# Chunked first stage, last gate on VectorE, and the order of work in the attention's tail and the second norm of a two-layer diffusion transformer

## The chip, the core and the metric

The kernel runs on one core of a Trainium2 chip. The engines are named as the profile names them: PE (TensorE, matrix products; PEld is its weight load), DVE (VectorE), ACT (ScalarE), POOL (GpSimd) and SP (SyncE, which here only issues transfers). The metric is the device time of one execution in microseconds.

## The reference

Two layers over 256 latent and 256 context tokens of 1024 columns. Each layer has a mixer (layer 0: retention with 4 heads; layer 1: neighbourhood attention with 32 heads) and an MLP of 4096 hidden columns. Six vectors per layer, shift, scale and gate for mixer and MLP, come from the condition `c` by a product with `ada_w` (adaLN).

```python
for i in range(DEPTH):
    mod = (silu_c @ ada_w[i] + ada_b[i])[:, None, :]
    mod_c = silu_cc @ ada_w[i] + ada_b[i]
    sh1, sc1, g1, sh2, sc2, g2 = jnp.split(mod, 6, axis=-1)
    ...
    h = x * (1.0 + sc1) + sh1
    hc = ctx * (1.0 + sc1c) + sh1c
    ...                                   # y, yc: retention (i = 0) or neighbourhood attention (i = 1)
    x = layer_norm(DN_ALPHA * x + g1 * y, ln_g[i, 0], ln_b[i, 0])
    h = x * (1.0 + sc2) + sh2
    x = layer_norm(DN_ALPHA * x + g2 * sq_relu_mlp(h, mlp_w1[i], mlp_w2[i]), ln_g[i, 1], ln_b[i, 1])
    if not last:
        ...                               # the same for ctx
```

Everything is float32.

## The kernel before

**Products.** A float32 operand is held as two parts that PE takes in its faster float32r form: a high part (`hi`, `hTh`: an ACT cast) and a low part (`lo`, `hTl`: DVE takes the high part from the raw value). A product is three matmuls, high x high, low x high, high x low (`mm3`). Weights are streamed by SP's queue in units of 512 KB. `fetch` loads a unit into one of four buffers (`raw`; the background's adaLN weights `rawa` use the same four) and casts it (`hi`, five buffers), `lows` makes the low parts that are still outstanding (`lo`, five buffers), `take` gives the next unit to its user. PSUM has eight banks (`bank`).

**Order.** Engines are called through wrappers (`pe`, `act`, `dve`, `pool`, `sp`). Where a wrapper's `on` is true, its instructions stay in the order in which they are written; elsewhere a scheduler orders them. Nearly every instruction is recorded at the wrapper's line, 84 before and 89 in the changed kernel, so rows are told apart by tile names.

**First stage** (to about 66 us). The shift and scale of layer 0 are made by quarters of 256 columns: `quarter_loads` brings the `ada_w` columns (`rawq`, 1-KB pieces) and the same columns of `x` and `ctx` (`R`), `quarter_rows` sums them over the 1024 rows of `ada_w` on PE (`pada`, with `cT` as the condition) and adds the biases on DVE (`row`, `brows`), `ada_columns` turns the row into columns by a small matmul with a constant (`mod`). A chunk is 128 columns: `chunk` transposes it (`pt`), `modulate_chunk` scales and shifts it, half on DVE and half on ACT, into `aff`, and `split` makes `hTh` and `hTl`. `quarter_q` and `quarter_v` accumulate the chunk's products into q (`pq`, two banks) and v (`pv`, four banks) of the first retention head. `crow` holds the rows of `c`, `c_ctx`, `ln_g` and `ln_b`, and one transpose turns them all (`pc`). `make_strip` builds the decay masks of the heads on ACT and DVE.

**Background adaLN.** The other shifts, scales and gates are made beside the main work by a generator that `bg(n)` advances by n steps. In a step DVE adds a 128x1024 slab of weights, times a column of the condition, to `acc` (`acc<-rawa,scol`), and after eight slabs PE folds the partitions (`pada<-acc,onecol`). For the two parts named in `on_pe` PE sums the slabs directly instead (`pada<-rawa,cT`); the last one, the gate of layer 1's MLP, is taken in steps 5 to 8 of the attention (`ADA`). `bg_max` limits how far the generator goes: to 79 steps in the first layer's MLP.

**Attention of layer 1** (810 to 1010 us). `STEPS` lists what goes with each step of heads: scores (`pqk`), `soften` (softmax, `s`), `flip` and `invert` (transposes `ppt`, `pt`; reciprocals of the sums, `rr`), `attend` (`pav`), `turned` (ACT's copy `rt<-pav` of the reciprocals, and what follows from it), and the output projection `wo` (`pnw`) where its heads are ready. The last two steps and the start of the projection are written out singly.

**Second norm of layer 1** (1010 to 1043 us). The two 128-token tiles are normalised one after the other. `direct` modulates the transposed tile straight from PSUM (`hTh`, and again as `aff` for `hTl`), `tok_part` makes the first MLP products of a tile by operand part (`p00`, `p01` for tile 0), `tok_block` all three parts of a block in turn (`p10`, `p11` for tile 1), `activate` squares the positive part and `turn_block` transposes it.

Of the kernel before, what the change touches and what calls it, by code (L numbers as in the profile page):

```python
# [39 lines left out]
def make_consts():  # L40
# [14 lines left out]
    add("sel", sel)  # L55
    inv = f(1.0) / (f(10000.0) ** (np.arange(0, 128, 2, dtype=f) / f(128.0)))
# [8 lines left out]
    add("pad", np.zeros((P, -sum(q.shape[1] for q in parts) % LINE)))  # L65
# [39 lines left out]
def kernel(  # L105
# [83 lines left out]
    for i in range(4):  # L189
        w_rows(WI, 256 * i, 256, 0, 256)  # L190
        w_rows(WI, 256 * i, 256, 2 * D, 512)
# [103 lines left out]
    cst = cpool.tile([P, CONSTS.shape[1]], F32, tag="cst", name="cst")  # L295
    crow = scr("crow")[:, :P]
    sp.dma_start(out=crow[0:8, :], in_=c.rearrange("a (k p) -> (a k) p", p=P))
    act.dma_start(out=crow[8:16, :], in_=c_ctx.rearrange("(k p) -> k p", p=P))
    sp.dma_start(out=cst[:], in_=consts)
    act.dma_start(out=crow[16:48, :], in_=ln_g.rearrange("l i (k p) -> (l i k) p", p=P))  # L300
    act.dma_start(out=crow[48:80, :], in_=ln_b.rearrange("l i (k p) -> (l i k) p", p=P))

    def cv(name, p0=0, p1=P):
        o, w = CONST_COLS[name]
        return cst[p0:p1, o : o + w]
# [6 lines left out]
    pc = bank("pc")  # L312
    pe.transpose(pc[:, 0:80], crow[0:80, :], ident[0:80, 0:80])
    act.activation(out=scol[:].rearrange("p a k -> p (a k)"), in_=pc[:, 0:16], func=AF.Silu)
    for t in range(2):
        dve.tensor_copy(
            out=cT[:, :, :, t], in_=scol[:, t, :].unsqueeze(2).broadcast_to([P, KC, 16])
        )
    dve.tensor_copy(out=lnT[:].rearrange("p a b c k -> p (a b c k)"), in_=pc[:, 16:80])


    lns = dram.tile([64, P], F32, tag="lns", name="lns")
    lsc = scr("lsc")
    pool.tensor_scalar_mul(out=lsc[0:80, :P], in0=crow[0:80, :], scalar1=ALPHA)
    act.dma_start(out=lns[:], in_=lsc[16:80, :P])

    mhalf = small(cpool, 1, "mhalf", name="mhalf")
    dve.memset(mhalf[:], -0.5)

    onecol = small(cpool, 33, "onecol", name="onecol")  # L330
    lgn = cpool.tile([P, 2, 8], F32, tag="lgn", name="lgn")
    lgm = small(cpool, 4, "lgm", name="lgm")
# [63 lines left out]
    def ada_quarter_load(i, ss):  # L396

        raws = []
        for kh in range(2):
            raw = slot(ss[kh], [P, 2, 4, 256], F32, "rawq")  # L400
            for s in range(2):
                w_ap = ada_w[0][512 * kh : 512 * kh + 512, s * D + 256 * i : s * D + 256 * i + 256]
                sp.dma_start(out=raw[:, s], in_=w_ap.rearrange("(k p) n -> p k n", p=P))
            raws.append(raw)
        return raws

# [46 lines left out]
    def on_pe(l, w, part):  # L453
        return (l, w, part) in ((0, 0, 2), (1, 1, 2))
# [38 lines left out]
    def bg_stream():  # L493
# [13 lines left out]
        for step, (l, w, part, offs, n) in enumerate(plan):  # L507
# [207 lines left out]
    pv = [bank("pv") for _ in range(4)]  # L715
    AQ = ((S_GS, S_SH), (S_SL, S_VH))

    def quarter_loads(i):
        raws = ada_quarter_load(i, AQ[i % 2])
        for a, src in enumerate((x, ctx_in)):  # L720
            cols = slice(256 * i, 256 * i + 256)
            sp.dma_start(out=RR[a][:, :, cols], in_=src[0][:, cols].rearrange("(t p) c -> p t c", p=P))
        return raws

    def quarter_ada(pr, raws, kh):
        for k in range(4 * kh, 4 * kh + 4):
            ada_mm(pr, k, P, lambda j: raws[kh][:, j // 2, k - 4 * kh, (j % 2) * P : (j % 2 + 1) * P])
# [11 lines left out]
    def strip_tables():  # L739
        sp.dma_start(  # L740
# [43 lines left out]
    def quarter_rows(i, raws):  # L784
        pr = bank("pada")
        for kh in range(2):
            quarter_ada(pr, raws, kh)
# [1266 lines left out]
```

## Time and profile before

| | |
|---|---|
| median of 3 runs | 1220.34 us (1220.25 to 1220.78) |
| the profiled execution | 1221.34 us, span 1219.6 us |
| granted clock of PE, mean | 0.996 |
| PE busy | 1191.1 us, 98% of the span |
| DVE / ACT / POOL busy | 809.3 / 477.3 / 209.2 us |
| moved by DMA | 194.54 MB, mean 160 GB/s |

The span is the time from the first to the last instruction that the profile shows; the execution's own time is 1.74 us longer. The chain of waits follows back from the last instruction to what released each one; the waits list sums, for each engine, the time that it stood and what ended it. A window row gives the length, each engine's busy time with its count of instructions, the granted clock, the DMA share and the GB/s. In a timeline row stand the start, the duration, the engine, the operation, and in brackets the idle time before it.

### The profile page before, as it was taken

What the parts mean: (1) busy time and instruction counts of PE and PEld (TensorE: products, weight loads), DVE (VectorE), ACT (ScalarE), POOL (GpSimd) and SP (SyncE); (2) the same over time, 40 slices, a digit from 0 to 9 for tenths busy, and PEclk for the clock granted to TensorE, in tenths of its full rate; (3) what the DMA queues carried; (4) which work ended last, traced back from release to release, by engine and by line L of the source; (5) the groups of instructions that cost most, each with busy time, mean ns of one, the idle gap of its engine ahead of it and who ended that gap; (6) DMA issues with size and microseconds to landing.
All of it is one profiled execution on the core that took longest, in us unless ns stands there. A gap on an engine that the chain in (4) does not pass through costs nothing.

```text
span 1219.6 us, 17977 instructions
## 1 busy us (share of the span) xinstructions
PE 1191.1 (98%) x6969; PEld 994.7 (82%) x6969; DVE 809.3 (66%) x1283; ACT 477.3 (39%) x806; POOL 209.2 (17%) x306
## 2 busy tenths in 40 slices
PE   6999999999999999999999999999999998999997
PEld 4777888888888889888888888889887877999886
DVE  2598857678685477667766664467575688776445
ACT  2462222323223246432123442137465565565341
POOL 2003501420340230000110000123244330000001
PEclk9999999999999999999999999999999999999999
DMA  9765443375653125327556556426256644566761
GB/s 312 228 211 184 138 151 108 105 253 132 137 155 121 57 69 143 113 91 222 169 183 213 178 177 219 146 64 204 66 148 186 182 139 123 173 210 191 233 207 38
DMA packets 145397, 194.54 MB, mean 160 GB/s; under 512 B 26808, under 2 KB 88480, under 8 KB 145312
## 3 DMA queue, kind: packets, MB, share of 16 engines
q1 hardware_dynamic: 139184, 181.12, 47.4%
q0 software_dynamic: 4544, 9.46, 2.9%
q10 hardware_dynamic: 1584, 2.81, 0.8%
q8 instruction: 54, 0.88, 0.3%
q14 instruction: 31, 0.25, 0.1%
HBM read 188.53 MB, written 5.75 MB: 159 GB/s over the span
## 4 chain that ended last, share of the span: by engine, by line
PE 87%; DVE 5%; DMA 3%; ACT 2%; issue 2%; POOL 1%; DVEq 0%; SPq 0%; ACTq 0%; POOLq 0%
PE p L84 42%; PE pv L84 7%; PE pq L84 7%; PE pw L84 7%; PE pg L84 6%; PE pn L84 4%; PE pnv L84 3%; PE pada L84 2%; PE po L84 2%; PE pS L84 1%; PE ppt L84 1%; DVE lo L84 1%; DMA rawa<-in_ada_w_dram 1%; PE pt L84 1%; PE pav L84 1%
## 5 line engine op out<-in xcount | busy, mean ns | idle before, releaser
L84 DVE TENSOR_TENSOR lo<-raw,hi 128x1024 fp32r<-128x1024 f32 (+1 forms) x227 | 275.2, 1221 | 149.5 <-ACT hi L84 149.1
L84 ACT CAST hi<-raw 128x1024 fp32r<-128x1024 f32 (+1 forms) x227 | 233.0, 1036 | 350.8 <-PE p L84 187.3
L84 PE MATMUL p<-hi,hid 128*128 128x512 f32 (+1 forms) x832 | 242.4, 374 | 0.0
L84 PEld LDWEIGHTS p<-hi,hid 128*128 128x128 f32 x832 | 152.2, 188 | 28.8 <-issue 1.2
L84 PE MATMUL p<-hTh,hi 128*128 128x256 f32 (+1 forms) x512 | 168.8, 330 | 0.2 <-ACT hTh L84 0.2
L84 PE MATMUL p<-hTh,lo 128*128 128x256 f32 (+1 forms) x512 | 168.3, 329 | 0.8 <-DVE lo L84 0.8
L84 PE MATMUL p<-hTl,hi 128*128 128x256 f32 (+1 forms) x512 | 168.3, 329 | 0.3 <-DVE hTl L84 0.3
L84 PE MATMUL p<-lo,hid 128*128 128x512 f32 (+1 forms) x416 | 155.3, 373 | 0.0
L84 POOL TENSOR_TENSOR R<-R,acc 128x512 f32<-128x512 f32 x40 | 66.9, 1682 | 297.8 <-DVE acc L84 297.7
L84 PEld LDWEIGHTS p<-hTh,hi 128*128 128x128 f32 x512 | 97.2, 190 | 9.8 <-issue 0.8
L84 PEld LDWEIGHTS p<-hTh,lo 128*128 128x128 f32 x512 | 96.4, 188 | 9.8 <-DVE lo L84 1.0
L84 PEld LDWEIGHTS p<-hTl,hi 128*128 128x128 f32 x512 | 96.4, 188 | 9.4 <-DVE hTl L84 0.8
L84 DVE SCALAR_TENSOR_TENSOR acc<-rawa,scol,acc 128x1024 f32<-128x1024 f32 x49 | 62.1, 1281 | 45.7 <-DMA rawa<-in_ada_w_dram 45.5
L84 PEld LDWEIGHTS p<-lo,hid 128*128 128x128 f32 x416 | 78.4, 188 | 13.5
L84 DVE SCALAR_TENSOR_TENSOR strips<-rawa,scol,strips 128x512 f32<-128x512 f32 x84 | 70.2, 885 | 5.3 <-DMA rawa<-in_ada_w_dram 5.3
L84 ACT CAST hid<-r 128x256 fp32r<-128x256 f32 (+1 forms) x64 | 32.0, 500 | 81.0 <-DVE r L84 81.0
L84 POOL TENSOR_TENSOR rstd<-rstd,mhalf 128x1 f32<-128x1 f32 x28 | 19.2, 686 | 247.5 <-DVE rstd L84 245.5
L84 ACT ACTIVATE s<-s,mn 128x512 f32<-128x512 f32 x64 | 45.5, 712 | 27.9 <-DVE mn L84 27.9
L84 DVE TENSOR_TENSOR hid<-r,hid 128x256 fp32r<-128x256 f32 (+1 forms) x64 | 34.6, 540 | 28.9 <-ACT hid L84 28.7
L84 PE MATMUL pq<-hTh,hi 128*128 128x512 f32 x128 | 49.9, 392 | 2.0 <-ACT hTh L84 2.0
L84 PE MATMUL pw<-hi,oh 128*128 128x512 f32 x128 | 51.2, 400 | 0.0
L84 PE MATMUL pw<-hi,ol 128*128 128x512 f32 x128 | 50.1, 392 | 1.1 <-DVE ol L84 1.1
(219 smaller groups left out, 2278.1 us busy)
## 6 DMA issues: line engine op xcount, KB each, us to landing
raw<-in_mlp_w_dram SPq DMA_DIRECT2D x128, 512.0 KB
rawa<-in_ada_w_dram SPq DMA_DIRECT2D x80, 512.0 KB
raw<-in_ret_w_in_dram SPq DMA_DIRECT2D x46, 512.0 KB
raw<-in_nat_w_in_dram SPq DMA_DIRECT2D x24, 512.0 KB
rawq<-in_ada_w_dram SPq DMA_DIRECT2D x16, 512.0 KB
raw<-in_ret_w_o_dram SPq DMA_DIRECT2D x16, 512.0 KB
bias<-rpb_rows POOLq DMA_DIRECT2D x32, 128.0 KB, 2.9
raw<-in_nat_w_o_dram SPq DMA_DIRECT2D x8, 512.0 KB
```

The source lines that it names most:

```text
L84: r = f(*args, **kwargs)
```

## The change

1. The first stage works by chunks of 128 columns. The first two chunks are loaded by themselves (`chunk_loads`, `rawq` in 512-byte pieces), the others in pairs (`pair_loads`, 1-KB pieces). The sums of a chunk go over four column groups (`chunk_sums`), the row is copied without bias, a matmul with a new constant `sel4` adds the groups and makes columns (`chunk_columns`), and the biases are added there as columns (`bcol`). `chunk_modulate` makes `hTh` straight from PSUM, then `aff` and `hTl`. The first two chunks' products go by operand part (`part_v`). Two groups of five matmuls on a tile of ones, `still`, stand ahead of the first product. Constants are loaded in two pieces, and the `ln` rows later. The strips take three DVE operations instead of five; the scaling of the residual `R` by ALPHA moves from DVE to ACT, behind `evac_v` of head 0. All of pe, act and dve keep the written order in this stage.
2. The last gate is no longer in `on_pe`: DVE sums it in the first MLP's second half (`bg_max` 87, `bg(2 + fp % 2)`), and `ADA` leaves the `STEPS`. Its row is stored by POOL's queue instead of SP's. The load of `gb`, which shares a slot with `acc`, waits for this gate's fold.
3. In the attention's last steps one `lo` moves from ahead of the copies `pt` to behind `soften` of the last step, and `turned` of the last step moves from behind the first projection products to right behind `flip`.
4. In the second norm `tok_block` goes: the second tile's products also go by operand part, with parts of the first tile's between them, and `direct` makes `aff` only when its low part is asked for.

The start on PE, before. `pc` is the turn of the rows, `pada` the sums of a quarter:

```order
L84 MATMUL pc_91<-cst,crow_82 128x80
L84 MATMUL pada_143<-rawq_130,cT 32x128 x16
L84 MATMUL pada_143<-rawq_133,cT 32x128 x16
L84 MATMUL pt_212<-cst,R_110 128x128 x2
L84 MATMUL pt_222<-cst,R_110 128x128 x2
L84 MATMUL pada_143<-cst,row_176 128x8
L84 MATMUL pt_212<-cst,R_111 128x128 x2
L84 MATMUL pt_222<-cst,R_111 128x128 x2
L84 MATMUL pq_122<-hTh,hi_183 128x512
L84 MATMUL pq_123<-hTh,hi_183 128x512
```

And after, where `pq<-still` are the matmuls on ones:

```order
L89 MATMUL pc_150<-cst_81,crow_83 128x16
L89 MATMUL pc_155<-cst_81,brow_2_84 128x16
L89 MATMUL pada_159<-rawq_120,cT 32x128 x8
L89 MATMUL pq_113<-still_115 128x256 x5
L89 MATMUL pada_159<-rawq_120,cT 32x128 x8
L89 MATMUL pt_184<-cst_81,R_101 128x128 x2
L89 MATMUL pada_159<-cst_81,R_102 128x128 x2
L89 MATMUL pada_159<-cst_81,row_173 128x2 x2
L89 MATMUL pq_113<-still_115 128x256 x5
L89 MATMUL pq_113<-hTh,hi_197 128x512
L89 MATMUL pq_114<-hTh,hi_197 128x512
```

The first product now follows 16 matmuls of sums and four transposes, where 32 and eight stood, with ten matmuls on ones between them, and the two parts that need only `hTh` come ahead of the part that needs `hTl`.

ACT at the end of the attention, before (`hilo` and `hi` are weights of the projection and the MLP):

```order
L84 COPY pt_6901<-ppt_8941 128x384
L84 CAST hilo_8955<-raw_8953 128x1024
L84 CAST hi_8960<-raw_8958 128x512
L84 CAST hi_8961<-raw_8958 128x512
L84 COPY rt_8982<-pav_6897 128x128
L84 CAST oTh_6898<-rt_8982 128x4x32
```

And after:

```order
L89 COPY pt_6988<-ppt_8975 128x384
L89 COPY rt_8987<-pav_6984 128x128
L89 CAST hilo_8991<-raw_8989 128x1024
L89 CAST hi_8996<-raw_8994 128x512
L89 CAST hi_8997<-raw_8994 128x512
L89 CAST oTh_6985<-rt_8987 128x4x32
```

The copy `rt` now stands ahead of the three casts instead of behind them. The `lo` that moves on DVE stands in the diff.

DVE in the second norm, from the normalised second tile on, before:

```order
L84 TENSOR_SCALAR xn_8966<-R_110,mv_9160,rstd_9162 128x512
L84 TENSOR_TENSOR lo_9153<-raw_9150,hi_9152 128x1024
L84 TENSOR_SCALAR hTh<-pt_9210,AB_8970 128x128 x4
L84 TENSOR_SCALAR aff_9223<-pt_9205,AB_8970 128x128 x4
L84 TENSOR_TENSOR lo_9158<-raw_9155,hi_9157 128x1024
L84 TENSOR_TENSOR hTl<-aff_9223,hTh 128x4x128
L84 TENSOR_TENSOR hTl<-aff_9224,hTh 128x4x128
```

And after:

```order
L89 TENSOR_SCALAR xn_9002<-R_101,mv_9194,rstd_9196 128x512
L89 TENSOR_TENSOR lo_9187<-raw_9184,hi_9186 128x1024
L89 TENSOR_SCALAR hTh<-pt_9248,AB_9006 128x128 x4
L89 TENSOR_TENSOR lo_9192<-raw_9189,hi_9191 128x1024
L89 TENSOR_TENSOR hTl<-aff_9262,hTh 128x4x128
L89 TENSOR_SCALAR aff_9261<-pt_9243,AB_9006 128x128 x4
L89 TENSOR_TENSOR hTl<-aff_9261,hTh 128x4x128
```

The second `lo` and one `hTl` now stand ahead of the four `aff` operations.

The core of the diff:

```diff
-    cst = cpool.tile([P, CONSTS.shape[1]], F32, tag="cst", name="cst")
+
+    NC0 = P + 8 + 4
+    cst0 = cpool.tile([P, NC0], F32, tag="cst0", name="cst0")
+    cst1 = cpool.tile([P, CONSTS.shape[1] - NC0], F32, tag="cst1", name="cst1")
     crow = scr("crow")[:, :P]
+    brow0 = scr("brow0")[:, :P]
     sp.dma_start(out=crow[0:8, :], in_=c.rearrange("a (k p) -> (a k) p", p=P))
     act.dma_start(out=crow[8:16, :], in_=c_ctx.rearrange("(k p) -> k p", p=P))
-    sp.dma_start(out=cst[:], in_=consts)
-    act.dma_start(out=crow[16:48, :], in_=ln_g.rearrange("l i (k p) -> (l i k) p", p=P))
-    act.dma_start(out=crow[48:80, :], in_=ln_b.rearrange("l i (k p) -> (l i k) p", p=P))
+    act.dma_start(out=cst0[:], in_=consts[:, 0:NC0])
+    act.dma_start(out=brow0[0:16, :], in_=ada_b[0][0 : 2 * D].rearrange("(r p) -> r p", p=P))
...
     def on_pe(l, w, part):
-        return (l, w, part) in ((0, 0, 2), (1, 1, 2))
+        return (l, w, part) == (0, 0, 2)
...
-                        (sp if on_pe(l, w, part) and l else pool).dma_start(
+                        pool.dma_start(
...
+    def chunk_ada(k):
+
+        raw = slot(AQ[k], [P, 2, KC, P], F32, "rawq")
+        for i in range(2):
+            w_ap = ada_w[0][:, i * D + P * k : i * D + P * k + P]
+            sp.dma_start(out=raw[:, i], in_=w_ap.rearrange("(k p) n -> p k n", p=P))
+        adas[k] = lambda i, kk: raw[:, i, kk, :]
...
+    def chunk_loads(k):
+        chunk_ada(k)
+        chunk_x(k)
+        ws[k] = Weights(k)
+
+    def pair_loads(k):
+        pair_ada(k)
+        chunk_x(k, 2)
+        for j in range(2):
+            ws[k + j] = Weights(k + j)
...
+    def turn_over(n):
+        for _ in range(n):
+            pe.matmul(pq[0][:, :256], lhsT=still[:, :P], rhs=still[:, :256], start=True, stop=True)
...
+    def chunk_sums(k, i):
+
+        if k not in prs:
+            prs[k] = bank("pada")
+        for kk in range(KC):
+            j = kk % 4
+            pe.matmul(
+                prs[k][32 * j : 32 * j + 32, tsl(i)],
+                lhsT=cT[:, kk, :, :].rearrange("p a t -> p (a t)"),
+                rhs=adas[k](i, kk),
+                start=(kk < 4),
+                stop=(kk >= 4),
+                tile_position=(0, 32 * j),
+            )
...
+    def chunk_modulate(k, between=lambda: None):
+
         tmp = scr("aff")
-        dve.tensor_scalar(
-            out=tmp[:, :NLAT], in0=pt[:, :NLAT], scalar1=m[:, 1, k, 0:1], scalar2=m[:, 0, k, 0:1],
-            op0=ALU.mult, op1=ALU.add,
-        )
-        act.activation(
-            out=tmp[:, NLAT:], in_=pt[:, NLAT:], func=AF.Identity, scale=m[:, 1, k, 1:2], bias=m[:, 0, k, 1:2]
-        )
-        split(tmp[:], hTh[:, k, :], hTl[:, k, :])
-
-    def quarter_q(k, kk, wq):
-        wh, wl = wq
-        for dc in range(2):
-            mm3(pq[dc][:], (wh[:, kk, tsl(dc)], wl[:, kk, tsl(dc)]), hs(k, 0, NT), k == 0, k == KC - 1)
-
-    def quarter_v(k, kk, wv):
-        wh, wl = wv
+        for e, a in ((act, 0), (dve, 1)):
+            modulated(e, hTh[:, k, KINDS[a]], pts[k][a], k, a)
+        between()
+        for e, a in ((act, 1), (dve, 0)):
+            modulated(e, tmp[:, KINDS[a]], pts[k][a], k, a)
+        dve.tensor_sub(out=hTl[:, k, :], in0=tmp[:], in1=hTh[:, k, :].bitcast(F32))
...
+    def part_v(k, a, b):
+        w, h = (ws[k].hi, ws[k].lo), hs(k, 0, NT)
         for t in range(4):
-            mm3(pv[t][:], hs(k, t * P, (t + 1) * P), (wh[:, kk, :], wl[:, kk, :]), k == 0, k == KC - 1)
-
-    pr, row = quarter_rows(0, raws)
-    ada_columns(0, 0, pr, row, P, 0)
-    wq, wv = quarter_weights(0)
-    raws = quarter_loads(1)
-    tabs = strip_tables()
+            pe.matmul(
+                pv[t][:], lhsT=h[a][:, tsl(t)], rhs=w[b][:, Weights.V],
+                start=(k == 0 and a == b), stop=False,
+            )
...
+    for k in range(2):
+        chunk_loads(k)
+    pair_loads(2)
+    for e in (act, dve, pe):
+        e.on = True
+    first_columns()
+    first_biases()
+    chunk_sums(0, 0)
+    turn_over(5)
+    chunk_row(0, tsl(0))
+    chunk_sums(0, 1)
+    chunk_row(0, tsl(1))
+    chunk_turn(0)
+    chunk_columns(0)
+    turn_over(5)
+    w = ws[0]
+    w.high(w.Q)
+    chunk_modulate(0, lambda: (w.high(w.V), w.low(w.Q)))
+    w.low(w.V)
+    pv = [bank("pv") for _ in range(4)]
+    chunk_q(0, ((0, 0), (1, 0)))
+    part_v(0, 0, 0)
+    chunk_q(0, ((0, 1),))
+
+    for k in range(KC):
...
+        if k == 1:
+            chunk_q(k, ((0, 0),))
+            part_v(k, 0, 0)
+            chunk_q(k, ((1, 0), (0, 1)))
+        elif k:
+            chunk_q(k)
+        if k < KC - 1:
+            for i in range(2):
+                chunk_sums(k + 1, i)
+            chunk_turn(k + 1)
+            ws[k + 1].high()
+            chunk_row(k + 1)
+            if k > 1:
+                ws[k + 1].low()
+        if k in (0, 2):
+            pair_loads(k + 4)
+        if k > 1:
+            chunk_v(k, (0, 1))
+        else:
+            part_v(k, 1, 0)
+        if k < KC - 1:
+            chunk_columns(k + 1)
+            chunk_modulate(k + 1, lambda: None if k > 1 else ws[k + 1].low())
+        if k > 1:
+            chunk_v(k, (2, 3))
+        else:
+            part_v(k, 0, 1)
+        if k == 1:
+            tabs = strip_tables(dt)
+        if 1 < k < 6:
...
-            rotate(pq, qkh[:, 0:2], qkl[:, 0:2])
+            rotate(pq, qkh[:, 0:2], qkl[:, 0:2], True)
             evac_v(pv, vh, vl)
+            act.on = True
+            for a in range(2):
+                act.mul(out=RR[a][:], in_=RR[a][:], mul=ALPHA)
+            act.on = False
...
-        bg_max[0] = 79
+        bg_max[0] = 87
...
-                bg(2)
+                bg(2 + fp % 2)
...
-            bg_until(79)
-            bg_max[0] = 200
+            bg_until(87)
             held = take(4)
             gb = slot(S_VL, [P, 2, D], F32, "gb")
...
-        (1, 1, 0, [V(0)], [ADA]),
-        (0, 0, 0, [V(1)], [ADA]),
-        (0, 0, 0, [V(2)], [REST, ADA]),
-        (0, 0, 0, [V(3)], [ADA]),
+        (1, 1, 0, [V(0)], []),
+        (0, 0, 0, [V(1)], []),
+        (0, 0, 0, [V(2)], [REST]),
+        (0, 0, 0, [V(3)], []),
...
-        lows(1 if n == len(STEPS) - 2 else 100)
+        lows(100 if n < len(STEPS) - 2 else len(STEPS) - 1 - n)
...
     soften(n)
+    lows(1)
...
     flip(n)
+    turned(n)
...
-    turned(n)
     attend(n)
...
-        for half in range(2):
-            part(half == 1, half, lambda k, i, half=half: tmps[half][:, tsl(i)])
 
         def low(half):
+            part(half == 1, half, lambda k, i: tmps[half][:, tsl(i)])
             ks = slice(4 * half, 4 * half + 4)
             dve.tensor_sub(
                 out=lo[:, ks], in0=tmps[half][:].rearrange("p (k t) -> p k t", k=4), in1=hi[:, ks].bitcast(F32)
             )
 
-        return [lambda half=half: low(half) for half in range(2)]
+        return low
...
+    HH, HL, LH = (0, 0), (0, 1), (1, 0)
+    tok_part(p00, 0, 0, *HH, LOW, start=True)
+    tok_part(p00, 0, 0, *HL, LOW)
+    tok_part(p00, 0, 0, *HH, HIGH)
+    tok_part(p00, 0, 0, *HL, HIGH)
+    tok_part(p00, 0, 0, *LH, LOW)
+    tok_part(p01, 0, 1, *HH, start=True)
+    tok_part(p01, 0, 1, *LH, LOW)
+    tok_part(p00, 0, 0, *LH, HIGH, stop=True)
     shift = shift_of(mv1, r1)
     center(1, 0, mv1, r1, x1)
     center(1, 1, mv1, r1, x1, shift)
     lows(1)
     pts1 = [mod_pt(x1, half) for half in range(2)]
-    tok_part(p01, 0, 1, 1, 0)
-    lo1 = direct(pts1, 1)
+    tok_part(p01, 0, 1, *LH, HIGH)
+    tok_part(p01, 0, 1, *HL, LOW)
+    low1 = direct(pts1, 1)
     lows(1)
-    tok_part(p01, 0, 1, 0, 1, stop=True)
-    for f in lo1:
-        f()
+    p10, p11 = [bank("p1t") for _ in range(2)]
+    tok_part(p10, 1, 0, *HH, start=True)
+    tok_part(p10, 1, 0, *HL)
+    tok_part(p01, 0, 1, *HL, HIGH, stop=True)
+    low1(1)
+    low1(0)
     fetch(1)
     r00 = activate(p00)
-    p10 = tok_block(1, 0)
+    tok_part(p10, 1, 0, *LH, HIGH)
+    tok_part(p11, 1, 1, *HH, start=True)
+    tok_part(p11, 1, 1, *HL)
+    tok_part(p10, 1, 0, *LH, LOW, stop=True)
     r01 = activate(p01)
+    tok_part(p11, 1, 1, *LH, stop=True)
...
-    p11 = tok_block(1, 1)
+    turn_block(r01, 0, 1)
     r10 = activate(p10)
     lows(1)
-    turn_block(r01, 0, 1)
     turn_block(r10, 1, 0)
     r11 = activate(p11)
```

More of the change, by code (lines that the diff above doesn't have):

```diff
@@ L323, with first_columns @@
[L323 to L327, printed above, removed]
+    bcol = cpool.tile([P, 2, KC], F32, tag="bcol", name="bcol")
+    lns = dram.tile([64, P], F32, tag="lns", name="lns")
+    def first_columns():
+        pc = bank("pc")
+        pe.transpose(pc[:, 0:16], crow[0:16, :], ident[0:16, 0:16])
+        act.activation(out=scol[:].rearrange("p a k -> p (a k)"), in_=pc[:, 0:16], func=AF.Silu)
+        for t in range(2):
+            dve.tensor_copy(
+                out=cT[:, :, :, t], in_=scol[:, t, :].unsqueeze(2).broadcast_to([P, KC, 16])
+            )
@@ L394, in ada_load @@
         return raw
[L396 to L405, printed above, removed]
     def ada_bias(l, offs, nb):
@@ L857 @@
+    act.on = dve.on = False
     pe.on = sp.on = False
```

230 lines of the change are left out of this document (125 added, 105 removed).

## The prediction

> **What bounds the kernel now.** I read the busy shares of the page first, then its chain, then the waits of TensorE (PE), then windows and timelines of the stages where PE isn't full.
>
> ```profile
> PE 1191.1 (98%) x6969; PEld 994.7 (82%) x6969; DVE 809.3 (66%) x1283; ACT 477.3 (39%) x806; POOL 209.2 (17%) x306
> PE 87%; DVE 5%; DMA 3%; ACT 2%; issue 2%; POOL 1%; DVEq 0%; SPq 0%; ACTq 0%; POOLq 0%
> ```
>
> PE is busy for 98% of the span and carries 87% of the chain. Time can be won in two ways only: less PE work, or less of the 28.5 us in which PE stands (span 1219.6 less 1191.1). The list of waits says where it stands longest:
>
> ```profile
> PE pc L84 <- DMA crow<-in_ln_b_dram: 5.7, 1, 5.7
> PE pada L84 <- DMA rawq<-in_ada_w_dram: 2.5, 2, 1.3
> PE p1t L84 <- DVE lo L84: 2.5, 1, 2.5
> PE pq L84 <- ACT hTh L84: 2.0, 1, 2.0
> ```
>
> The start (crow, rawq, hTh) holds 10.2 us and the second norm (p1t) 2.5; two waits at the end of the attention, shown below, hold 2.5 more. The diff edits all of these. Its gate edit is different: it takes work off PE where PE doesn't wait.
>
> **First stage.** The chain of the start, in order of time:
>
> ```profile
> 5.62 6.51 DMA rawq<-in_ada_w_dram
> ...
> 16.32 1.02 ACT aff L84 x2
> 17.34 0.52 ACT hTh L84
> 17.90 2.71 PE pq L84 x6
> ...
> 50.64 1.00 PE pada L84 x28
> ...
> 52.76 0.44 PE pt L84 x4
> 53.20 0.12 PE pada L84 x2
> ...
> 59.37 2.73 PE pv L84 x12
> ...
> 64.86 1.15 PE pv L84 x5
> ```
>
> Before, the first product starts at 17.90, after a whole quarter of the adaLN weights, and the stage's last product ends at 66.0. After, it needs one chunk of 128 columns: 1.05 MB of adaLN weights, 0.26 of x and context, 0.39 of q and v weights; 1.70 MB. What the queues carry, in windows (the last column is GB/s, ahead of it the DMA share and the granted clock):
>
> ```profile
> 2.00:4.00 2.00, 0.00 (x0) 0.00 (x0) 0.00 (x0) 0.37 (x1) 0.00 (x0) 1.00 0.77 197
> 4.00:6.00 2.00, 0.27 (x1) 0.18 (x1) 0.00 (x0) 0.92 (x1) 0.21 (x1) 1.00 1.03 325
> 6.00:8.00 2.00, 0.74 (x5) 0.19 (x4) 0.50 (x3) 0.18 (x1) 0.36 (x1) 1.00 1.14 283
> 30.00:45.00 15.00, 15.00 (x121) 11.08 (x120) 6.93 (x13) 6.36 (x11) 0.57 (x3) 1.00 1.06 344
> 18.00:20.50 2.50, 2.50 (x6) 1.27 (x6) 2.25 (x3) 2.48 (x3) 0.00 (x0) 0.65 1.09 347
> 20.50:25.00 4.50, 4.50 (x45) 2.71 (x44) 0.15 (x1) 0.32 (x2) 1.12 (x1) 0.82 1.08 356
> ```
>
> Moved are 0.39 MB by 4 us, 1.04 by 6 and 1.61 by 8; at 344 GB/s the chunk with 0.1 MB of constants is in by 8.6, say landed by 9. Modulating and casting took 1.6 us in the chain (16.32 to 17.90). First product: 10.5.
>
> A chunk then costs PE 18 products of 512 columns at 2.73/12 = 0.228, 4.1 us; 32 records of sums at 1.00/28, 1.15; four transposes, 0.44; four records of columns, 0.24: 6.0 us with gaps. The clock of 0.65 and 0.82 in the first 7 us of products cost 0.35 x 2.5 + 0.18 x 4.5 = 1.7 us before; the ten added matmuls on `still` keep PE busy ahead of the first product, so I leave that out. Chunks 0 and 1 are through at 22.5. Four chunks and constants are 6.9 MB: 1.61 by 8 us, the rest at 347 GB/s in 15.2, landed by 24.1; so PE stalls 1.6. Six chunks of 6.0 follow, less 1.8 of sums and turns that the last doesn't have: 58.3. That would gain 7.7.
>
> But 1.31 of the 1.70 MB of an early chunk come in 512-byte pieces, where the quarters' came in 1 KB, and no row has such pieces alone. The nearest are the windows from 4 to 8 us, in which 0.26 MB of bias rows in 512-byte pieces were among the rest: 325 and 283 GB/s against 344 are 0.16 MB short, as if these pieces ran at 0.26/0.42 = 62% of the rate. At 62% an early chunk takes 1.31/0.344 x 0.61 = 2.3 us more, and the gain is 3.1. At 50% it is 3.8 a chunk, and the gain is 0.1. I take 5.0, about midway between 62% and the full rate, since other small loads of the start share the shortfall. Ends: 0 and 7.7.
>
> The Trainium skill, "DMA: Bandwidth & Descriptors", Specifications, gives 512 bytes as the smallest transfer that still runs at line rate. By that page the stage gains 7.7 instead of 5.0; the two windows lean the other way, and no run shown here has the pieces alone.
>
> Behind the stage two ALPHA scalings of 128x2048 move from DVE to ACT:
>
> ```profile
> L84 ACT CAST hi<-raw 128x1024 fp32r<-128x1024 f32 (+1 forms) x227 | 233.0, 1036 | 350.8 <-PE p L84 187.3
> 66.00:80.00 14.00, 13.92 (x78) 10.24 (x77) 13.77 (x29) 9.17 (x18) 0.00 (x0) 1.00 0.32 100
> ```
>
> At twice 1036 ns each they take 4.1 us; ACT has 4.8 free there, and DVE, full at 13.77 of 14, is relieved. If one delays a `qkh` cast by its whole length PE loses 2.1; if DVE's relief tells, something is won. I take nothing; ends -2 and +1.
>
> **The gate on VectorE.** Four groups of sums leave PE in the attention; eight DVE operations and a fold (four matmuls, eight records) come into the first MLP's second half:
>
> ```profile
> 926.86 1.05 PE L84 MATMUL pada<-rawa,cT 128*32 128x256 f32 x16
> ...
> 957.89 1.05 PE L84 MATMUL pada<-rawa,cT 128*32 128x256 f32 x16
> 958.87 0.97 PE L84 MATMUL pqk<-kT,qT 32*128 32x512 f32 x12
> L84 DVE SCALAR_TENSOR_TENSOR acc<-rawa,scol,acc 128x1024 f32<-128x1024 f32 x49 | 62.1, 1281 | 45.7 <-DMA rawa<-in_ada_w_dram 45.5
> 727.22 0.64 PE L84 MATMUL pada<-acc,onecol 128*32 128x256 f32 x8
> 640.00:670.00 30.00, 30.00 (x136) 24.91 (x135) 20.75 (x24) 9.27 (x13) 1.83 (x4) 1.00 0.65 215
> 760.00:790.00 30.00, 30.00 (x139) 24.26 (x138) 12.19 (x15) 6.06 (x6) 6.02 (x4) 1.00 0.51 162
> ```
>
> A group holds PE 0.98 us (957.89 to 958.87) with the next product right behind it: 4 x 0.98 = 3.9 of pure work. DVE's 8 x 1.281 = 10.2 us fall where it has 9.3 of 30 free (640) to 17.8 (760), and PE is at 30.00 of 30.00. The eight loads of 512 KB that move there, 4.2 MB, go beside a DMA share of 0.65. The fold costs 0.5. Net 3.4; ends 2, if some weights come late, and 3.9. The load of `gb` on SP, which now waits for the last fold with weight loads queued behind it, is covered by the four weights already taken; without them it would be one of these late weights. The row's transfer passes from SP to POOL and nobody waits for it before the attention's end.
>
> **End of the attention.**
>
> ```profile
> 1000.70 0.33 PE L84 MATMUL pav<-cst,rr 128*128 128x128 f32 x1 [0.98 <-DVE rt L84]
> ...
> 1004.37 1.25 DVE L84 TENSOR_TENSOR lo<-raw,hi 128x1024 fp32r<-128x1024 f32 x1
> ...
> 1007.22 1.06 ACT L84 CAST hilo<-raw 128x1024 fp32r<-128x1024 f32 x1
> ...
> 1009.21 0.28 ACT L84 COPY rt<-pav 128x128 f32<-128x128 f32 x1
> ...
> 1009.53 0.49 PE L84 MATMUL pav<-pt 128*128 128x128 f32 x2 [1.52 <-DVE hilo L84]
> ```
>
> The 1.52 is named after DVE's `hilo`, but PE goes on 0.04 after ACT's copy `rt` ends at 1009.49, and that copy stood behind the cast of 1007.22 and two more. Ahead of them it is done 2 us earlier, and this wait goes. The 0.98 goes since a `lo` of 1.25 no longer stands ahead of `rt`; but that `lo` is only moved, to beside the one of 1004.37, ahead of the next reciprocals, so most of the 0.98 comes back one step later. I take 1.2; ends 0.3 and 2.5.
>
> **Second norm.**
>
> ```profile
> 1031.31 1.36 DVE L84 TENSOR_SCALAR hTh<-pt,AB 128x128 fp32r<-128x128 f32 x4
> 1033.87 1.22 DVE L84 TENSOR_TENSOR lo<-raw,hi 128x1024 fp32r<-128x1024 f32 x1
> 1035.14 0.74 PE L84 MATMUL p1t<-lo,hTh 128*128 128x256 f32 x4 [2.46 <-DVE lo L84]
> 1035.00:1037.00 2.00, 1.86 (x11) 1.86 (x12) 2.00 (x6) 0.82 (x3) 0.00 (x0) 0.73 0.28 74
> 1037.00:1039.40 2.40, 2.40 (x14) 2.40 (x13) 1.08 (x1) 1.04 (x1) 0.00 (x0) 0.51 0.51 166
> ```
>
> PE waits 2.46 us for hi x low products, whose `lo` (ended 1035.09) stood behind `aff`; then it runs at a clock of 0.73 and 0.51, which costs 0.27 x 1.86 + 0.49 x 2.4 = 1.7. After, that `lo` stands ahead of `aff`, and the second tile's products, which need `hTh` alone (ended 1032.67), fill the time until it is there. DVE's chain is not shorter: the `aff` of 1.36 is late next, but its products come last. Gain up to 4.2; I take 4.0 for a short wait at the new start. Ends: 2.3 (the clock still falls) and 5.
>
> The Trainium skill, "TensorE: Matmul & The Clock Gate", Part 1, has the clock fall after an idle window of about 3.4 us. By that rule a wait of 2.46 would not slow PE and removing it would be worth 2.5 here, the sum 1.5 less; the 0.51 of the trace, after a shorter wait, disagrees, and it decides.
>
> **The sum.** 5.0 + 0 + 3.4 + 1.2 + 4.0 = 13.6. The stages follow one another on a PE that is otherwise full, so I add the terms. The profiled execution took 1221.34 (span 1219.6 and 1.7 around it), 1.0 above the median of the runs; 1221.34 less 13.6 is 1207.7, and against the median 1206.7.
>
> **Rivals.**
> - Small pieces run at half rate: the first stage gains about 0, the total 8.6, so 1211.7. For it: the windows of 4 to 8 us; against: the bias rows were repeated reads of few rows, and other small loads ran beside.
> - All terms at their good ends, 7.7 + 3.9 + 2.5 + 5 = 19.1: 1201.2. For it: PE follows every released wait in the rows; against: the moved `lo`, and the windows just named.
> - The other side: the first MLP's second half starves. Each fourth-gate load takes one of the weights' four raw buffers, and its DVE operation, waiting in order for its transfer, holds the `lo`s behind it. The page's `acc` row has 45.5 us of DVE idle on `rawa` already, 0.9 an operation, with PE uncovered nowhere. The kernel is slower by over 2.4 us (0.2%, about the least that a measurement here tells from no change) if PE loses 16.0, that is 2.0 at each of the eight operations, beyond what the prepared weights cover. At 2.5 each, 20 are lost: 1226.7. A product of 512 columns over four tiles gives PE 24 x 0.228 = 5.5 us a weight unit and DVE needs 1.22 for it (1004.37), so cover is there.
> - The change doesn't do what it says: pairs of columns come late as well, `lo` and the ACT copy stand where they stood for PE, and only the gate's 3.4 and 1 or so of the norm are left: 1216.
>
> **How the numbers follow.** Forecast (1203.5 to 1210) 0.55; half rate 0.2; all good 0.13; change without effect 0.07, half of it within 0.2%; starving 0.05, most of it slower. The range that leaves out 2 in 10 reaches from the all-good case, 1201, to a little past the half rate, 1214; the unknown rate of 512-byte pieces alone makes 7.7 us of it. Faster 0.93, same 0.03, slower 0.04.
>
> **What would show it.** First stage: the first `pq` at about 10.5 us, a PE wait of 1 to 2 us on `rawq` near 23, the first 10 us at 340 GB/s (near 200 to 250 would mean slow pieces), the stage's last `pv` near 61. Gate: no `pada<-rawa` group after 900, `acc` x57, no PE wait between 640 and 810. Attention: no `pav` wait over 0.5. Second norm: no 2.46, clock 1.00 throughout, and 4 us less from the `pt` transposes to the next MLP. I would be wrong most likely in the first stage, by the rate of its transfers, or by a DVE that can't feed six chunks at 6.0 us each while it makes the strips.

## The result and the profile after

| | before | after |
|---|---|---|
| median of 6 runs | 1220.56 us (1219.52 to 1223.38) | 1213.82 us (1209.92 to 1215.33) |
| ratio to before | | 0.9938, 95% interval 0.992 to 0.9955 |
| the profiled execution | 1221.34, span 1219.6 | 1214.56, span 1212.6 |

The kernel is faster by 0.6%, some 7 us, where 13.6 were forecast. The time lies inside the range, half way between the forecast and no change. The busy shares and the chain of the page after:

```profile
PE 1191.6 (98%) x6949; PEld 996.0 (82%) x6949; DVE 823.7 (68%) x1298; ACT 482.0 (40%) x809; POOL 211.7 (17%) x307
PE 88%; DVE 6%; ACT 3%; DMA 2%; issue 1%; POOL 1%; DVEq 0%; SPq 0%; ACTq 0%; POOLq 0%
```

PE is as busy as before (1191.6 against 1191.1 us), although the gate's sums left it; it stands 21.0 us instead of 28.5. So part of the time in which it no longer stands is now spent in slower work, as the landmarks below show. The first rows of the list of PE's waits after:

```profile
PE pc L89 <- DMA cst<-in_consts_dram: 4.7, 1, 4.7
PE pt L89 <- DVE r L89: 2.1, 1, 2.1
PE pc L89 <- DMA brow<-in_ada_b_dram: 1.5, 1, 1.5
PE pav L89 <- DVE rt L89: 1.0, 1, 1.0
```

Gone are `rawq`, `p1t` on `lo`, `pq` on `hTh` and the 1.5 of `pav`. New are a wait of 2.1 of a transpose on `r`, the squared block, and one of 1.5 on the bias rows (`brow`) ahead of the first sums.

Where the time came from is read by landmarks: the start of the same products in both profiles. Each row here is worked out from the first or last start that the two traces give for a tile.

| landmark | before | after | gained so far | gained in between |
|---|---|---|---|---|
| first product (`pq`) | 17.9 | 12.9 | 5.0 | 5.0 |
| first product behind the first stage | 66.1 | 64.5 | 1.6 | -3.4 |
| first MLP starts | 456.5 | 454.0 | 2.5 | 0.9 |
| attention starts (`pn`) | 818.5 | 816.8 | 1.6 | -0.9 |
| its last `pn` | 986.4 | 981.5 | 4.9 | 3.3 |
| second norm's products start (`p1t`) | 1024.5 | 1018.4 | 6.1 | 1.2 |
| the last of them starts | 1043.0 | 1032.5 | 10.5 | 4.4 |
| second MLP starts (`p`) | 1043.5 | 1035.5 | 8.0 | -2.5 |
| its last `p` | 1211.4 | 1204.8 | 6.6 | -1.4 |

Two places give back what was won just ahead of them: the first stage behind its first product, and the second MLP's start. The first, in PE's timeline of the kernel after (from chunk 0 on, the starts of each chunk's first products and what stands between two of them):

```profile
6.38 0.28 PE L89 MATMUL pc<-cst,brow 16*128 16x16 f32 x1 [1.46 <-DMA brow<-in_ada_b_dram]
6.59 1.08 PE L89 MATMUL pada<-rawq,cT 128*32 128x128 f32 x16
7.60 1.44 PE L89 MATMUL pq<-still 128*128 128x256 f32 x5
8.97 1.08 PE L89 MATMUL pada<-rawq,cT 128*32 128x128 f32 x16
...
12.88 1.05 PE L89 MATMUL pq<-hTh,hi 128*128 128x512 f32 x2
...
20.53 0.70 PE L89 MATMUL pq<-hTh,hi 128*128 128x512 f32 x2
...
26.02 1.17 PE L89 MATMUL pv<-lo,hTh 128*128 128x512 f32 x4
27.08 0.70 PE L89 MATMUL pq<-hTh,hi 128*128 128x512 f32 x2
27.86 0.73 PE L89 MATMUL pq<-hTh,lo 128*128 128x512 f32 x2
29.11 0.73 PE L89 MATMUL pq<-hTl,hi 128*128 128x512 f32 x2 [0.52 <-DVE hTl L89]
...
34.49 0.62 PE L89 MATMUL pq<-hTh,hi 128*128 128x512 f32 x2
...
40.78 0.62 PE L89 MATMUL pq<-hTh,hi 128*128 128x512 f32 x2
```

Sixteen records of sums take 1.01 us here (6.59 to 7.60), where 32 take it later; a product of 512 columns takes 0.43 at 12.88 and 0.23 from about 16: PE runs at half pace. Chunk 0 takes 7.65 us, chunk 1 6.55, chunk 2 7.41, the next four 6.3, 6.3, 6.6 and 6.5. From the bias rows at 6.38 to chunk 2's first product at 27.08 the list has no wait of PE: its own queue sets this stretch.

The second place, first ACT and then PE and the clock (windows) behind the second norm:

```profile
1031.89 1.99 ACT L89 CAST hi<-raw 128x1024 fp32r<-128x1024 f32 x2 [1.21 <-PE p1t L89]
1033.79 0.63 ACT L89 CAST hid<-pt 128x256 fp32r<-128x256 f32 x2
1034.31 0.39 ACT L89 ACTIVATE r<-p1t 128x256 f32<-128x256 f32 x1
```

```profile
1032.60 0.60 PE L89 MATMUL pt<-cst,r 128*128 128x128 f32 x4
1035.32 0.44 PE L89 MATMUL pt<-cst,r 128*128 128x128 f32 x2 [2.12 <-DVE r L89]
```

```profile
1033.00:1036.00 3.00, 0.88 (x8) 0.68 (x7) 1.82 (x4) 1.91 (x5) 0.00 (x0) 1.00 0.56 175
1036.00:1040.00 4.00, 4.00 (x24) 4.00 (x23) 4.00 (x6) 1.39 (x3) 0.00 (x0) 0.57 0.50 144
```

The squaring of block (1, 0) on ACT, at 1034.31, stands behind two weight casts and two turned blocks. PE waits for it, and then runs at a clock of 0.57. Before, DVE had finished this block at 1042.4, and PE's own products ran until 1043.1, so PE didn't wait for it.

### The profile page after: what moved, and what is told of

It is laid out like the page before. It is cut to its first block, busy times and chain, and to the rows that moved or that the text cites. A ratio compares the mean times of both kernels' runs of the same rounds, so it can differ in the third digit from the quotient of the medians.

```text
span 1212.6 us, 17987 instructions
## 1 busy us (share of the span) xinstructions
PE 1191.6 (98%) x6949; PEld 996.0 (82%) x6949; DVE 823.7 (68%) x1298; ACT 482.0 (40%) x809; POOL 211.7 (17%) x307
## 4 chain that ended last, share of the span: by engine, by line
PE 88%; DVE 6%; ACT 3%; DMA 2%; issue 1%; POOL 1%; DVEq 0%; SPq 0%; ACTq 0%; POOLq 0%
PE p L89 42%; PE pq L89 7%; PE pv L89 7%; PE pw L89 6%; PE pg L89 6%; PE pn L89 5%; PE pnv L89 4%; PE pada L89 2%; PE po L89 2%; PE ppt L89 1%; PE pS L89 1%; PE pqk L89 1%; DMA rawa<-in_ada_w_dram 1%; DVE lo L89 1%; PE pav L89 1%
## 5 line engine op out<-in xcount | busy, mean ns | idle before, releaser
L89 DVE TENSOR_TENSOR lo<-raw,hi 128x1024 fp32r<-128x1024 f32 (+2 forms) x228 | 277.2, 1223 | 148.0 <-ACT hi L89 147.2
L89 ACT CAST hi<-raw 128x1024 fp32r<-128x1024 f32 (+2 forms) x228 | 233.6, 1033 | 355.1 <-PE p L89 187.8
L89 PE MATMUL p<-hTl,hi 128*128 128x256 f32 (+1 forms) x512 | 169.1, 330 | 0.4 <-DVE hTl L89 0.4
L89 DVE SCALAR_TENSOR_TENSOR acc<-rawa,scol,acc 128x1024 f32<-128x1024 f32 x56 | 71.1, 1281 | 32.8 <-DMA rawa<-in_ada_w_dram 32.7
L89 POOL TENSOR_TENSOR rstd<-rstd,misc 128x1 f32<-128x1 f32 x28 | 19.1, 684 | 228.3 <-DVE rstd L89 226.3
L89 PE MATMUL pg<-hi,hTh 128*128 128x512 f32 x128 | 51.3, 401 | 0.0
```

The source lines that it names most:

```text
L89: r = f(*args, **kwargs)
```

## The experiments

**Undoing one part each.** Each of these kernels is the changed one with one part as before.

`u_first`: the first stage, with the strips and the ALPHA scaling.

```diff
-    for k in range(2):
-        chunk_loads(k)
-    pair_loads(2)
+    raws = quarter_loads(0)
...
+    for i in range(4):
+        k = 2 * i
+        quarter_q(k, 0, wq)
...
```

> The kernel before with the gate, attention and second-norm parts of the change, the first stage as before. Theory A (the new first stage is bound by PE itself: its queue runs sums, ten matmuls on ones and turns one after the other at half clock, and a chunk costs 6.3 us instead of 6.0): the part is worth what the profile after shows up to the end of head 0, about 2.2 us, so this comes to about 1216. Rival (the part is worth the 5.0 forecast and something later gave 3 back): about 1219, and the landmarks behind the first stage then stand 5 us later than in the profile after.

Measured: 0.9957 (0.9941 to 0.9973), 1217.21 us. The changed kernel stood at 0.9938, and in a second series (`after_again`, below) at 0.9948; so the part is worth 1.1 to 2.3 us, not 5. Its landmarks agree: first product behind the stage at 66.2 instead of 64.5, first MLP at 455.9 instead of 454.0. Its profiled execution is the fastest of the six (1212.6), at the quick pace and without the low clock that are described below; so the landmarks size the part, and not this execution's time.

`u_norm`: the second norm.

```diff
-    tok_part(p10, 1, 0, *HH, start=True)
-    tok_part(p10, 1, 0, *HL)
-    tok_part(p01, 0, 1, *HL, HIGH, stop=True)
+    tok_part(p01, 0, 1, 0, 1, stop=True)
...
+    p10 = tok_block(1, 0)
```

> The changed kernel with the second norm as before. Theory B (the new order ends the second norm's products 4.4 us sooner, but PE then waits 2.1 us for the squared block r and runs 1.3 to 1.7 us longer at a low clock, so nearly all is given back): within 1 us of the changed kernel, about 1214.5. Rival (the norm part is worth the 4.0 forecast, the loss lies elsewhere): about 1217.8.

Measured: 0.9936 (0.992 to 0.9953), 1213.68 us: the same as the changed kernel. The profile has the old wait and the low clock back, and no wait on `r`:

```profile
1029.68 0.79 PE L89 MATMUL p1t<-lo,hTh 128*128 128x256 f32 x4 [2.50 <-DVE lo L89]
1030.00:1033.00 3.00, 3.00 (x17) 3.00 (x16) 2.62 (x5) 0.39 (x1) 0.00 (x0) 0.54 0.59 175
```

So the part exchanges one wait with a low clock behind it for another with the same, and Theory B holds for the kernel after. The two totals may mix executions of both paces, and the profile of `u_norm` has the quick pace of the second MLP (below), so the stretch from the first `p1t` to the last `p` is the better measure. With both kernels at the slow pace it takes 186.9 us before and 186.4 after: 0.5 won. At the quick pace it takes 184.1 in `u_norm` and 182.4 in `u_first`, `u_tail` and `no_warm`, which have the new order and the wait on `r`, but a clock of 1.00 behind it: 1.7 won where the clock doesn't fall.

`u_gate`: the gate on PE in the attention.

```diff
-        return (l, w, part) == (0, 0, 2)
+        return (l, w, part) in ((0, 0, 2), (1, 1, 2))
...
-        bg_max[0] = 87
+        bg_max[0] = 79
```

> The changed kernel with the last gate on PE in the attention again. The landmarks of the two profiles put the gate part at 3.1 us in the attention, less 0.9 that the first MLP takes longer: 2.2 to 2.3 net, so about 1216.2. Rival (the 3.4 forecast holds and the MLP's 0.9 is something else): about 1217.4, with the first MLP as long as in the changed kernel.

Measured: 0.9968 (0.9956 to 0.998), 1216.43 us: the part is worth 2.4 to 3.7 us by the two series. From the first `pn` to the first `p1t` it takes 204.8 us against 201.6, from the first MLP's start to the first `pn` 362.2 against 362.9: 3.2 less 0.7, a net 2.5. The runs alone don't tell 2.3 from 3.4; the landmarks stand nearer to 2.3.

`u_tail`: the end of the attention.

```diff
     flip(n)
-    turned(n)
...
+    turned(n)
     attend(n)
```

> The changed kernel with the end of the attention as before. Theory C (the wait behind the casts goes, the one of 0.98 moves): the part is worth 1.2 to 1.5, so about 1215.3, and the waits on rt of 1.0 and behind hilo of 1.5 both stand in the profile. Rival (the moved lo gives all back): 1214, the same as the changed kernel.

Measured: 0.9952 (0.994 to 0.9965), 1213.87 us; by the ratios 0.5 to 1.7 us more than the changed kernel, by the landmarks (first `pn` to first `p1t`, 202.9 against 201.6) 1.4. Both waits are there:

```profile
996.77 0.33 PE L89 MATMUL pav<-cst,rr 128*128 128x128 f32 x1 [0.98 <-DVE rt L89]
1005.61 0.49 PE L89 MATMUL pav<-pt 128*128 128x128 f32 x2 [1.52 <-DVE hilo L89]
```

The kernel after has one:

```profile
1001.49 0.33 PE L89 MATMUL pav<-cst,rr 128*128 128x128 f32 x1 [0.96 <-DVE rt L89]
```

It is the one of the next step: the 1.52 went for good, the 0.98 moved on, as 0.96.

**The new wait taken away.** In `turn` two lines move together, so what each does alone isn't shown. By the program, `load_gate` issues its transfer on ACT's queue outside the wrapper, so it isn't held in the written order, and the next cast, which is held only behind that transfer, is free to go ahead of the turned blocks. With the load earlier, the casts stay behind.

```diff
+    G2 = load_gate(1, 1, 1)
     r00 = activate(p00)
...
+    r10 = activate(p10)
     turn_block(r00, 0, 0)
     turn_block(r01, 0, 1)
-    r10 = activate(p10)
...
-    G2 = load_gate(1, 1, 1)
```

> The changed kernel with two lines moved: the gate's load ahead of the squaring of tile 0 (so that ACT keeps the written order, two weight casts come behind the turned blocks) and the squaring of block (1, 0) ahead of the turns of tile 0. Theory B: the wait of 2.1 on r falls below 0.5 and with it the low clock after it, together 3 to 4 us: about 1210.2. Rival (the wait is set by PE's own products or by the weights, and the clock falls by itself): the wait stays or moves to p on lo, and the time stays at 1213 to 1214.

Measured: 0.992 (0.9908 to 0.9932), 1211.85 us (1210.59 to 1212.37). The wait on `r` is gone, 0.30 of `p` on `lo` is left, and the clock stays:

```profile
1036.00:1040.00 4.00, 3.70 (x33) 3.55 (x32) 4.00 (x6) 2.52 (x4) 0.00 (x0) 1.00 0.62 193
```

From the last product of the second norm to the last `p` it takes 169.1 us instead of 172.4, both at the slow pace. Theory B's mechanism is shown; the total fell by 2 to 3.4 us by the two series of the changed kernel.

**The start.** `no_warm` drops the matmuls on ones.

```diff
     chunk_sums(0, 0)
-    turn_over(5)
...
     chunk_columns(0)
-    turn_over(5)
```

> The changed kernel without the ten matmuls on ones. Theory A (they stand on PE's path at half clock, the first five for 1.4 us, and do not raise the clock in time): the first product starts 0.8 to 1.4 us sooner, about 11.5 to 12.1, and the total falls by as much, about 1212.6. Rival (they bring the clock up sooner for the first chunk): the first product is sooner, but chunk 0 takes longer than its 7.65 us, and the total stays or rises by up to 1.5.

Measured: 0.9924 (0.9909 to 0.9939), 1212.1 us. The first product starts at 12.61, in spite of bias rows that landed 0.8 later; but chunk 0 takes 8.2 us, and chunk 2 starts at 27.36 instead of 27.08. In the first stage nothing is won. The first MLP starts at 453.9 against 454.0, so the lower total comes from elsewhere: from the first `p1t` to the last `p` its profile takes 182.4 us against 186.4, by the clock, which didn't fall here, and the pace (below).

`best` is `turn` and `no_warm`, with the bias rows turned behind the first sums:

```diff
     first_columns()
-    first_biases()
     chunk_sums(0, 0)
...
     chunk_turn(0)
+    first_biases()
     chunk_columns(0)
```

> The two moved lines of the run 'turn', no matmuls on ones, and the transpose of the bias rows behind the first chunk's sums and turns instead of ahead of them. Theory A: PE no longer waits 1.5 to 2.2 us for the bias rows with the sums behind that wait, the first product starts at 10.7 to 11.3 instead of 12.9, and the total is about 1.5 to 2 below 'turn': 1210. Rival (the start is set by the landing of the first adaLN pieces, or the clock stays low for longer): first product after 12, total as 'turn', 1211.9.

Measured: 0.9929 (0.9916 to 0.9941), 1211.4 us. The first product starts at 11.79, 1.1 sooner than in the kernel after, and chunk 2 at 27.24, 0.2 later. Theory A falls in this: what is taken out of PE's queue ahead of the first product isn't won, since the half pace then lasts longer (chunk 0 takes 8.9 us here). Over eleven profiles with this stage the first product starts between 11.8 and 13.7, and chunk 2 between 26.5 and 27.9. An early start of chunk 2 goes with an early end of the half pace. In `u_gate`, `after_again` and `turn_lo` PE left it ahead of the first product, and chunk 2 starts between 26.5 and 26.8; in the other eight it did so later, and chunk 2 starts at 27.1 or later. In `u_gate` chunk 0 took 6.31 us, but chunk 1 7.54: PE now waited for chunk 2's columns of `x` and `ctx`, which it has to turn there.

```profile
23.07 0.44 PE L89 MATMUL pt<-cst,R 128*128 128x128 f32 x2 [0.33 <-DMA R<-in_x_dram]
23.83 0.44 PE L89 MATMUL pada<-cst,R 128*128 128x128 f32 x2 [0.32 <-DMA R<-in_ctx_dram]
```

`after_again` and `turn_lo` wait 0.3 for the same columns, the other eight not at all. So two floors lie close together: the half pace, and the landing of chunk 2.

`all_512` loads all chunks singly, in 512-byte pieces.

```diff
-    pair_loads(2)
+    for k in (2, 3):
+        chunk_loads(k)
...
-            pair_loads(k + 4)
+            for j in range(2):
+                chunk_loads(k + 4 + j)
```

> The changed kernel with all eight chunks loaded singly, in 512-byte pieces. If these pieces run at nearly the full rate, the windows from 12 to 40 us show 320 to 350 GB/s and the stage ends within 0.5 us of the changed kernel's 64.6. Rival of the prediction (62% of the rate): about 220 to 240 GB/s, a chunk takes 7.2 us to load against 6.3 on PE, and the stage ends near 69 or later.

Measured once: 1213.25 us. Its windows, and then one of the kernel after, which has 1-KB pieces there:

```profile
12.00:20.00 8.00, 8.00 (x59) 6.51 (x60) 3.22 (x7) 2.37 (x4) 0.00 (x0) 1.00 1.16 310
20.00:30.00 10.00, 9.41 (x72) 6.41 (x70) 5.87 (x11) 4.49 (x8) 0.00 (x0) 1.00 1.16 304
```

```profile
20.00:30.00 10.00, 9.41 (x75) 6.11 (x77) 5.54 (x10) 5.15 (x8) 3.10 (x2) 1.00 1.09 356
```

A chunk of 1.70 MB at 307 GB/s takes 5.54 us; its 0.39 MB of weights take 1.10 at 356, so the 1.31 MB in small pieces take 4.44: 295 GB/s, 83% of the rate. That is neither the full rate nor 62%. The first product behind the stage starts at 65.3, 0.8 later than in the kernel after, and the stage's first product already started 0.7 later; so the small pieces cost next to nothing.

**Chunk 2 and the last small wait.** `turn_lo` is `turn` with a low part of weights moved ahead of the turned blocks; `turn_lo_start` adds that chunk 2's low part is made ahead of its columns.

```diff
     r10 = activate(p10)
+    lows(1)
     turn_block(r00, 0, 0)
     turn_block(r01, 0, 1)
-    lows(1)
```

> The run 'turn' with the low part of the second MLP's second weight unit made ahead of the turned blocks on DVE, so that PE's wait of 0.30 on it goes. In the profiles so far the 128x256 products of this MLP's first half run at one of two paces for some 75 us, 0.1133 or 0.1177 us from start to start, and the pace mostly changes where PE is interrupted (the wait of 0.30, the two transposes of r behind the first 48 products). Theory D (an interruption switches the pace): without the wait the products begin slow and go on fast behind the transposes, 2.7 to 2.9 us won beside the 0.3: about 1208.7. Rival (the pace is drawn anew in each execution): two groups of times 3 us apart; rival (nothing but the wait): 1211.5.

Measured: 0.9919 (0.9906 to 0.9932), 1211.33 us. The 0.30 is gone. Theory D's forecast falls: the pace does change at the transposes, but the other way. The products start at the quick pace (0.1136 us over the first 48) and go on at the slow one (0.1178).

```diff
-            if k > 1:
+            if k > 0:
                 ws[k + 1].low()
```

> The run 'turn_lo' with the low part of chunk 2's weights made ahead of the chunk's columns on DVE, as it is for chunks 3 to 7. Theory E (chunk 2 takes 7.4 us instead of 6.3 because PE waits in it for this low part and for hTl behind it): the step from the first product of chunk 2 to that of chunk 3 falls to 6.3 to 6.5, and the total is 0.9 to 1.1 below 'turn_lo'. Rival (chunk 2 waits for the landing of its weights at 24 to 25 us): the step stays at 7.4, same total.

Measured: 0.9916 (0.9903 to 0.9929), 1210.71 us (1210.5 to 1211.36), the fastest of all. Chunk 2 takes 6.81 us (27.87 to 34.68) instead of 7.41, so theory E holds for 0.6 of its 1.1; in the total it can't be told from `turn_lo`.

`extra_turn` puts two idle transposes into the second MLP of `turn`.

```diff
+            if f4 == 1 and f2 == 1:
+                px = bank("pt")
+                for i in range(2):
+                    pe.transpose(px[:, tsl(i)], r11[:, tsl(i)], ident)
```

> The run 'turn' with two more transposes, whose result nobody reads, behind the second 96 products of the second MLP: 0.3 us more work on PE. Theory D: the pace, slow behind the first transposes in 'turn' (0.1177), switches to 0.1133 there and the total falls by 2 to 2.5 us, about 1209.5. Rival (interruptions don't set the pace): 0.3 longer, about 1212.1.

Measured: 0.992 (0.9908 to 0.9932), 1211.74 us; the pace stays at 0.1178 on both sides of the two transposes, so an interruption alone doesn't switch it. Theory D falls here too.

`after_again` is the changed kernel, unchanged.

> The changed kernel as it is, for a second profile of it beside these runs. Theory D: the pace depends on where PE stood and may differ between two executions, since the waits in front of it depend on transfers and on the clock; the times spread over 5 us again around 1214. If the pace belongs to the kernel, the profile again shows 0.1177 and the clock low from 1036 to 1040.

Measured: 0.9948 (0.9936 to 0.996), 1214.52 us (1212.75 to 1216.77). The profile again shows the wait of 2.1, the clock at 0.66 from 1036 to 1041, and 0.1178.

## Why the prediction was right or wrong

- **What bounds the kernel** was right: PE carries the chain, and the time won is time in which PE no longer stands.
- **First stage: 5.0 forecast, 1.6 at its end.** This is the term that was most mis-sized, and not for the reason that the range was made for: the small pieces ran at 83% of the rate and decided nothing. Chunk 2's weights even landed about when forecast (ACT casts them at 24.17, as soon as they are there; 24.1 was forecast), but PE wasn't ready for them. The step that failed is "so I leave that out", of the half pace: the ten matmuls on ones run at half pace themselves, and it lasted to about 16 us, into chunk 0. The first product came at 12.9 instead of 10.5, chunks 0 and 1 took 14.2 us instead of 12.0, and the stall of 1.6 on chunk 2's weights didn't come: chunk 2 started at 27.1, 3.0 later than the 24.1 of the forecast. No run took the half pace away by itself, so how much of these 3.0 it holds is read from the eleven profiles and not shown. A second step failed behind it, "Six chunks of 6.0 follow". Chunk 2 took 7.4, since PE waited for its low part and `hTl` (0.6 of this went in `turn_lo_start`), and the next four took 25.7 instead of 24.0. Together 58.3 + 3.0 + 1.4 + 1.7 + 0.1 = 64.5. A steady chunk costs 6.3 to 6.6, and a quarter's two cost 12.9 before (32.66 to 45.52): the new stage isn't cheaper for PE, it only starts sooner. Over the eleven profiles its end lies between 63.8 and 65.4, against 66.1 before. Behind it 0.9 more was won up to the first MLP's start, where nothing was forecast and +1 was the end. `u_first`, which has the old scaling by ALPHA, wins 0.8 of it too, and the profiles with the new stage spread over 0.9 us in this stretch; so the move to ACT isn't shown to be worth anything.
- **Gate: 3.4 forecast, 2.3 to 2.5 in the profiles.** The mechanism was right, and DVE hid its eight operations, with no wait of PE between 640 us and the attention; the starving rival didn't come. The attention gave 3.2 (`u_gate`) where 3.9 of work left, and the first MLP took 0.9 longer (0.7 against `u_gate`) where the fold was 0.5. What the rest of these two differences is was not traced.
- **End of the attention: 1.2 forecast, 1.2 to 1.4.** Right in size and mechanism, in both halves: the wait named after `hilo` was ACT's copy, and the 0.98 came back a step later. The forecast's own sign, "no `pav` wait over 0.5", went against this and was wrong.
- **Second norm: 4.0 forecast, 4.4 at its last product, 0.5 at the last `p`** (the table, and `u_norm`). The wait of 2.46 and the low clock behind it went as foretold. The failed step is "its products come last", of what is late next: it looked at `aff` alone and stopped at the norm's products. Behind them PE needs the squared block of the second tile, whose ACT part now stood behind two casts; before, it was ready ahead of PE's last product. Where the clock stayed up behind this wait, 1.7 was won, still not 4.0. The order of the casts ahead of the turned blocks could have been read from the changed program.
- **The sum** took the terms as independent. In the first stage and the second norm, PE's gain ran into the next thing that was late, within 10 us of the place. The likeliest band (1203.5 to 1210) missed. The range held by luck: its upper end, 1214, was set for small pieces at half rate, which didn't come, and other losses of about the same size took that place.
- **The rule on the clock.** The prediction set "TensorE: Matmul & The Clock Gate", Part 1, of the Trainium skill (an idle window of about 3.4 us) against the trace's 0.51 behind 2.46 us. The runs stay with the trace, and add that it isn't certain: with the same wait of 2.1 on `r` the clock fell in the kernel after, `after_again`, `u_gate` and `all_512`, and stayed at 1.00 in `u_first`, `u_tail` and `no_warm`.

## What to carry to other kernels

Where one engine is full, cost a removed wait through to the next thing that the engine needs, on every engine's queue, and not only to the end of the edited stage. Read that queue in the changed program, since an instruction outside the written order can let others past it. An earlier start is worth only what the transfers and the clock behind it let through: here 5 us at the first product were 1.6 at the stage's end. The two moved lines and the two earlier low parts beat both kernels: `turn_lo_start` takes 0.9916 of the time before, the change alone 0.9938 to 0.9948.

## What the runs showed that I had not expected

- At the start PE runs at half pace while the clock column says 1.00 (0.43 us for a product of 512 columns at 12.88, and 1.00 in the window 10 to 15). It left that pace between about 11 us (`u_gate`) and 17.4 (`best`), in other executions of nearly the same program, with or without the matmuls on ones.
- The 128x256 products of the second MLP's first half run at one of two paces for 75 us, 0.1133 or 0.1178 us from start to start, which is about 2.8 us in all. Two windows, of the kernel after and of `no_warm` (PE's count is the one in the first brackets):

```profile
1060.00:1070.00 10.00, 10.00 (x88) 10.00 (x87) 9.33 (x14) 5.71 (x12) 0.00 (x0) 1.00 0.71 228
1060.00:1070.00 10.00, 10.00 (x91) 10.00 (x90) 9.05 (x15) 5.50 (x12) 0.00 (x0) 1.00 0.73 233
```

  The quick pace was in `u_first`, `u_norm`, `u_tail`, `no_warm` and `all_512`, the slow one in the others. No run moved a kernel from one to the other on purpose, and no profile pair of one kernel shows both, so its cause stays open. The times speak for a difference between executions, without showing it: the six of `no_warm` fall into two groups, 1210.3 to 1210.7 and 1213.5 to 1214.4, with mean granted clocks of 0.998 to 0.999 in both, and the profile, at the quick pace, is of the faster group. It is as large as most effects studied here, which is why the parts are sized by landmarks ahead of it and the totals only bound them.
